# Eight experts' two-layer MLP on one core: float32 tokens loaded per expert beside the weights, and the last three experts regrouped by layer

## The chip, the core and the metric

The kernel runs on one core of a Trainium2 chip. The metric is the device time of one execution in microseconds (us); before the change the median of three runs is 189.09 us (189.03 to 189.41). The profile is one further execution, taken by the hardware profiler: its span, from the first to the last instruction, is 187.0 us. A core has TensorE (PE, matrix multiplication, with weight loads listed apart as PEld), VectorE (DVE), ScalarE (ACT), GpSimd (POOL) and SyncE (SP, which here only issues transfers). Data moves between the memory of the chip and the core's SBUF through 16 DMA engines, which the queues of all issuing engines share.

## The reference

```python
n_experts, capacity, hidden, expert_hidden = 8, 256, 512, 2048
def reference(x, w1, w2):          # all float32
    h = np.matmul(x, w1)           # [8,256,512] x [8,512,2048]
    h = np.maximum(h, 0)
    return np.matmul(h, w2).astype(np.float32)   # x [8,2048,512]
```

Each expert has 256 tokens of its own, a first weight matrix of 512 by 2048 and a second of 2048 by 512. In float32 each weight matrix is 4.19 MB, and the tokens of all experts together are another 4.19 MB. So seventeen portions of that size are read, and 4.19 MB are written.

## The kernel before

The work is cut into 128 rows (P). Everything is multiplied in bfloat16 and accumulated in float32 in PSUM.

*Loads.* Loads of x and of the weights are all issued by GpSimd, on one queue, and the transfer itself turns float32 into bfloat16. The order is x of all experts in one transfer (L47), and then for each expert its w1 (L52) and its w2 (L55). The last expert's w2 comes in four pieces (L58). The pool of weight tiles holds four w1 and four w2, so the load for expert e waits until the layer of expert e-4 that reads the same buffer is done.

*Transposes.* [...] All of x is transposed once, ahead of the first expert: 64 transposes of 128x128 (L72), gathered by eight into a PSUM tile, and eight copies to `xt_sb`, shared between VectorE (L82) and ScalarE (L80).

*First layer of expert e* (L91). There are eight groups of eight matmuls, each 128 columns of w1 against the 256 tokens. A group fills one of four PSUM tiles `pt_h`. The relu takes it to `ht_sb` in bfloat16, on ScalarE for even groups (L101) and on VectorE for odd ones (L99).

*Second layer of expert e* (L111). Two PSUM tiles `pt_o`, one for each half of the tokens, are accumulated over sixteen blocks of the inner dimension: 32 matmuls of 128x512. VectorE copies one half out (L119), ScalarE the other (L120). SyncE issues the store (L122). For the last expert each half has a store of its own (L124 on SyncE, L125 on ScalarE).

*Order.* Each engine carries out its own instructions in the order in which they stand in its program, and waits on semaphores. That order isn't simply the order of the source: [...] In the kernel before, the order that results on TensorE is the plain one, first layer and second layer of each expert in turn.

## Time and profile before

| | before |
|---|---|
| device time, median of 3 | 189.09 us |
| span of the profile | 187.0 us |
| TensorE matmuls busy | 133.5 us (71%) |
| VectorE busy, ScalarE busy | 32.6 us (17%), 29.1 us (16%) |
| read from memory, written | 71.30 MB, 4.19 MB |
| first layers: 512 matmuls, L91 | 60.6 us |
| second layers: 256 matmuls, L111 | 66.7 us |
| median from issue to landing, weight tile | 73.4 us |
| median from issue to landing, store of one expert | 15.1 us |

The table is read with one thing in mind: a busy share is an average over the whole span. The time from issue to landing includes the time that a transfer stands behind others in its queue; a weight tile's 73 us say that it is issued several tiles ahead, not that it takes that long to move. The profile's waits tell which engine stood still for what, and the chain of waits tells what the end of the run depended on.

### The profile page before, as it was taken

The page shows a single profiled execution, that of the slowest core. Times are in us where ns is not written, and L with a number is a line of the kernel's source. Part 1 is how long each engine was busy: PE and PEld are TensorE (multiplying, and loading weights), DVE is VectorE, ACT ScalarE, POOL GpSimd, SP SyncE. Part 2 cuts the span into 40 slices and gives each one's busy share as a digit, 9 for nine tenths or more (in the row PEclk, how much of TensorE's full clock was granted, in tenths as well). Part 3 has the DMA queues.
Part 4 walks back from the last instruction along what each step waited for, and adds up shares of the span by engine and source line. Part 5 has one row for each costly group of instructions (what it writes and reads, how often), then busy time and mean ns, then how long its engine had stood idle before and what let it go on. Part 6 is the DMA issues. An engine that isn't in the chain of part 4 may idle for free.

```text
span 187.0 us, 1874 instructions
## 1 busy us (share of the span) xinstructions
PE 133.5 (71%) x832; PEld 91.0 (49%) x832; DVE 32.6 (17%) x44; ACT 29.1 (16%) x45; POOL 11.4 (6%) x26
## 2 busy tenths in 40 slices
PE   0009399786949493899749992999659492979990
PEld 0009388335934293348713592348624491339740
DVE  0005404010410122002400141003300041012201
ACT  2004413011210131003200131003200230012201
POOL 7301000010010101001100200001000000000000
PEclk9999969996999999589966998599999999699999
DMA  4999999999999999999999999999999999999902
GB/s 70 214 221 224 224 217 214 203 210 235 215 273 214 207 241 223 240 224 217 214 245 221 224 244 231 239 200 207 258 245 225 213 234 226 224 207 233 236 18 112
DMA packets 4182, 39.95 MB, mean 214 GB/s; under 512 B 464, under 2 KB 464, under 8 KB 2128
## 3 DMA queue, kind: packets, MB, share of 16 engines
q0 software_dynamic: 2880, 35.65, 90.1%
q1 hardware_dynamic: 1152, 3.93, 5.6%
q10 hardware_dynamic: 144, 0.26, 0.4%
q8 instruction: 6, 0.10, 0.2%
HBM read 71.30 MB, written 4.19 MB: 404 GB/s over the span
## 4 chain that ended last, share of the span: by engine, by line
PE 60%; DMA 22%; another core or an unknown queue 14%; issue 1%; POOL 1%; ACT 0%; POOLq 0%
PE pt_o L111 32%; PE pt_h L91 28%; DMA w_sb<-in_w_dram 22%; POOL x_sb L47 0%; ACT out_sb L120 0%; POOL w_sb L52 0%; POOL identity masks.py:197 0%; POOL w_sb L55 0%; POOLq L140 0%
## 5 line engine op out<-in xcount | busy, mean ns | idle before, releaser
L111 PE MATMUL pt_o<-w_sb,ht_sb 128*128 128x512 bf16 x256 | 66.7, 426 | 22.3 <-DMA w_sb<-in_w_dram 22.3
L91 PE MATMUL pt_h<-xt_sb,w_sb 128*128 128x256 bf16 x512 | 60.6, 281 | 12.6 <-DMA w_sb<-in_w_dram 12.6
L91 PEld LDWEIGHTS <-w_sb 128*128 128x128 bf16 x512 | 57.4, 146 | 17.4 <-DMA w_sb<-in_w_dram 16.1
L111 PEld LDWEIGHTS <-ht_sb 128*128 128x128 bf16 x256 | 27.5, 107 | 59.6 <-issue 37.1
L99 DVE TENSOR_SCALAR ht_sb<-pt_h 128x512 bf16<-128x512 f32 x32 | 22.1, 692 | 52.4 <-PE pt_h L91 52.4
L101 ACT ACTIVATE ht_sb<-pt_h 128x512 bf16<-128x512 f32 x32 | 19.1, 597 | 46.6 <-PE pt_h L91 46.6
L119 DVE COPY out_sb<-pt_o 128x512 f32<-128x512 f32 x8 | 5.5, 692 | 81.6 <-PE pt_o L111 81.6
L120 ACT COPY out_sb<-pt_o 128x512 f32<-128x512 f32 x8 | 4.7, 588 | 91.0 <-PE pt_o L111 91.0
L72 PE MATMUL pt_tr<-identity,x_sb 128*128 128x128 bf16 x64 | 6.5, 296 | 14.0 <-DMA x_sb<-in_x_dram 14.0
L72 PEld LDWEIGHTS <-x_sb 128*128 128x128 bf16 x64 | 6.3, 141 | 14.0 <-DMA x_sb<-in_x_dram 14.0
L82 DVE COPY xt_sb<-pt_tr 128x1024 bf16<-128x1024 bf16 x4 | 4.9, 1225 | 16.4 <-PE pt_tr L72 16.4
L52 POOL DMA_DIRECT2D w_sb<-in_w_dram x8 | 4.4, 544 | 44.3 <-PE pt_h L91 44.3
L80 ACT COPY xt_sb<-pt_tr 128x1024 bf16<-128x1024 bf16 x4 | 4.0, 1012 | 15.5 <-PE pt_tr L72 15.5
L55 POOL DMA_DIRECT2D w_sb<-in_w_dram x7 | 3.8, 546 | 38.7 <-PE pt_o L111 30.5
L58 POOL DMA_DIRECT2D w_sb<-in_w_dram x4 | 2.1, 532 | 32.0 <-DMA w_sb<-in_w_dram 19.3
L80 ACT ACT_TABLE_LOAD x1 | 1.3, 1283 | 0.7 <-PEq L140 0.7
L47 POOL DMA_DIRECT2D x_sb<-in_x_dram x1 | 0.7, 664 | 0.8 <-POOLq L140 0.8
masks.py:199 POOL TENSOR_SCALAR_AFFINE_SELECT identity<-identity 128x128 bf16<-128x128 bf16 x1 | 0.3, 333 | 0.1
masks.py:197 POOL MEMSET identity<- 128x128 bf16 x1 | 0.2, 244 | 0.0
L140 POOL MEMSET const-float32-0.0<- 128x1 f32 x1 | 0.1, 99 | 0.2 <-issue 0.2
L140 POOL MEMSET const-bfloat16-1.0<- 128x1 bf16 x1 | 0.1, 102 | 0.0
L140 POOL MEMSET const-uint8-127<- 128x1 uint8 x1 | 0.1, 102 | 0.0
(1 smaller groups left out, 0.1 us busy)
## 6 DMA issues: line engine op xcount, KB each, us to landing
w_sb<-in_w_dram POOLq DMA_DIRECT2D x15, 2048.0 KB, 73.4
out_dram<-out_sb SPq DMA_DIRECT2D x7, 512.0 KB, 15.1
x_sb<-in_x_dram POOLq DMA_DIRECT2D x1, 2048.0 KB, 12.7
w_sb<-in_w_dram POOLq DMA_DIRECT2D x1, 768.0 KB, 66.0
w_sb<-in_w_dram POOLq DMA_DIRECT2D x1, 640.0 KB, 69.7
w_sb<-in_w_dram POOLq DMA_DIRECT2D x1, 384.0 KB, 61.4
w_sb<-in_w_dram POOLq DMA_DIRECT2D x1, 256.0 KB, 52.4
out_dram<-out_sb SPq DMA_DIRECT2D x1, 256.0 KB, 2.0
```

The costliest lines, as they stand in the source:

```text
L52: nc.gpsimd.dma_start(a[:], w1_r[e])
L55: nc.gpsimd.dma_start(b[:], w2_r[e])
L58: nc.gpsimd.dma_start(b[:, lo:hi, :], w2_r[e, :, lo:hi, :])
L72: nc.tensor.transpose(pt[:, j2, :], x_sb[:, j2 * MT + mt, kt::KT1], identity[:])
L80: nc.scalar.copy(dst, src)
L82: nc.vector.tensor_copy(dst, src)
L91: nc.tensor.matmul(pt[:, i, :], w1_sb[e][:, kt, 2 * g + i::KT2], xt_sb[:, kt, e, :], start=(kt == 0), stop=(kt == KT1 - 1),)
L99: nc.vector.tensor_relu(ht_sb[:, 2 * g:2 * g + 2, :], pt[:])
L101: nc.scalar.activation(ht_sb[:, 2 * g:2 * g + 2, :], pt[:], mybir.ActivationFunctionType.Relu,)
L111: nc.tensor.matmul(po[mt][:], ht_sb[:, kt, mt * P:(mt + 1) * P], w2_sb[e][:, kt, :], start=(kt == 0), stop=(kt == KT2 - 1),)
L119: nc.vector.tensor_copy(out_sb[:, 0, :], po[0][:])
L120: nc.scalar.copy(out_sb[:, 1, :], po[1][:])
```

## The change

The tokens are no longer loaded whole and cast by the transfer. Each expert's tokens come as a float32 tile on SyncE's queue (`load_x`), four experts ahead, beside the weights on GpSimd's queue. `first_layer` casts the tile to bfloat16 on ScalarE, transposes it (eight transposes) and copies the result out of PSUM on VectorE, ahead of the expert's first layer. This is meant to let the weights start at once, without 4.19 MB of x ahead of them, and to take the transposes out of the beginning.

The order of layers is written in a list. For experts 0 to 4 it is first layer, second layer, as before. For the last three it is the first layers of experts 5, 6 and 7 and then their second layers, and the loads follow the same list. It is meant to have only second layers left when the last weights arrive. The pool of hidden tiles grows from two to four buffers for this. Last, the final four matmuls of the last expert are reordered so that the first half of its tokens is finished two matmuls earlier.

The core of the diff:

```diff
-    x_sb = const.tile([P, J, H], bf, name="x_sb")
-    nc.gpsimd.dma_start(x_sb[:], x_r)
...
-    hpool = ctx.enter_context(tc.tile_pool(name="hidden", bufs=2))
+    xpool = ctx.enter_context(tc.tile_pool(name="xs", bufs=AHEAD))
+    tpool = ctx.enter_context(tc.tile_pool(name="xts", bufs=2))
+    hpool = ctx.enter_context(tc.tile_pool(name="hidden", bufs=4))
...
+    def load_x(e):
+        x_sb[e] = xpool.tile([P, MT, H], f32, tag="x", name="x_sb")
+        nc.sync.dma_start(x_sb[e][:], x_r[e])
...
+    def first_layer(e):
+        x_bf = tpool.tile([P, MT, H], bf, tag="xb", name="x_bf")
+        nc.scalar.copy(x_bf[:], x_sb[e][:])
+        pt = ps_o.tile([P, KT1, MT, P], bf, tag="ps_o", name="pt_tr")
         for kt in range(KT1):
+            for mt in range(MT):
                 nc.tensor.transpose(
+                    pt[:, kt, mt, :], x_bf[:, mt, kt::KT1], identity[:]
                 )
+        xt = tpool.tile([P, KT1, C], bf, tag="xt", name="xt_sb")
+        nc.vector.tensor_copy(xt[:], pt[:].rearrange("p k m q -> p k (m q)"))
...
+        if last:
+            order = order[:-4] + [(kt, mt) for mt in range(MT) for kt in (KT2 - 2, KT2 - 1)]
...
+    order = []
+    for e in range(E - 3):
+        order += [(1, e), (2, e)]
+    order += [(1, e) for e in range(E - 3, E)] + [(2, e) for e in range(E - 3, E)]
+
+    for e in range(AHEAD):
+        load_x(e)
+    for layer, e in order:
+        (load_w1 if layer == 1 else load_w2)(e)
...
+    for layer, e in order:
+        if layer == 1:
+            first_layer(e)
+        else:
+            second_layer(e)
+            if e + AHEAD < E:
+                load_x(e + AHEAD)
```

## The prediction

> **What bounds the kernel now.** I read the page's slices first, then the chain of waits, then TensorE's timeline, and last the stretches between landings. The slices, 4.675 us each:

> ```profile
> PE   0009399786949493899749992999659492979990
> DMA  4999999999999999999999999999999999999902
> GB/s 70 214 221 224 224 217 214 203 210 235 215 273 214 207 241 223 240 224 217 214 245 221 224 244 231 239 200 207 258 245 225 213 234 226 224 207 233 236 18 112
> ```

> The DMA row is full from the second slice to the 38th; TensorE's row has holes everywhere. The transfers set the pace until about 178 us, and what comes after is a tail. The chain of waits shows the tail:

> ```profile
> 158.50 8.75 PE pt_o L111 x32
> 167.26 0.99 another core or an unknown queue
> 168.25 0.04 issue
> 168.29 7.21 PE pt_h L91 x64
> 175.50 6.92 PE pt_o L111 x32
> 182.42 0.02 issue
> 182.44 0.59 ACT out_sb L120
> ```

> At 168.25 the last w1 lands. From there TensorE works without a stop: 7.21 + 6.92 us. The last weights land near 178 us while it is still busy, so the end hangs on the landing before last, plus two layers. From the last matmul (182.42) to the end of the span (187.0) are 4.58 us of eviction, store and closing.

> TensorE's timeline shows how a layer's length depends on the idle time ahead of it (in brackets):

> ```profile
> 55.17 7.07 PE L111 MATMUL pt_o<-w_sb,ht_sb 128*128 128x512 bf16 x32 [2.61 <-DMA w_sb<-in_w_dram]
> 75.49 9.87 PE L111 MATMUL pt_o<-w_sb,ht_sb 128*128 128x512 bf16 x32 [3.66 <-DMA w_sb<-in_w_dram]
> 95.84 9.93 PE L111 MATMUL pt_o<-w_sb,ht_sb 128*128 128x512 bf16 x32 [3.32 <-DMA w_sb<-in_w_dram]
> 147.60 7.20 PE L91 MATMUL pt_h<-xt_sb,w_sb 128*128 128x256 bf16 x64 [2.75 <-DMA w_sb<-in_w_dram]
> 158.50 8.75 PE L111 MATMUL pt_o<-w_sb,ht_sb 128*128 128x512 bf16 x32 [3.69 <-DMA w_sb<-in_w_dram]
> ```

> The same 32 matmuls take 7.07 us after 2.6 us of idling and up to 9.93 us after more than 3.3: the clock had been halved. The stretches between landings (length, busy times by engine, clock, DMA share, GB/s written) give the price of a weight tile:

> ```profile
> 147.56:158.46 10.90, 7.20 (x64) 7.04 (x65) 2.77 (x4) 2.39 (x4) 0.00 (x0) 1.00 1.02 240
> 158.46:168.25 9.79, 8.75 (x32) 3.46 (x31) 0.69 (x1) 0.59 (x1) 0.00 (x0) 0.83 0.97 206
> ```

> A tile takes 9.8 us; the stretch that also carries a store takes 10.9, so a store of 0.52 MB costs 1.1.

> [...]

> **The change part by part.**

> *Bytes.* Nothing is saved: x is read as 4.19 MB of float32 either way. In before x is one portion on the queue of the weights, about 9.8 us. As plain float32 it moves like the stores do. By stretches that is 8 x 1.1 = 8.8 us; by the page's queue table the 3.93 MB of q1 took 5.6% of 187 us, so 4.19 MB take 11.2. I take 10.0, that is +0.2, and keep -1.0 and +1.4.

> *Start.* SyncE is released at about 0.7 us, GpSimd issued x at 1.23. I take -0.5 us (bounds 0 and -1.2, as the first GB/s show in before only after 2.5 us).

> *Casts, transposes, copies.* Eight casts on ScalarE: nearest row L80, 128x1024 at 1.01 us, so 8.1 us instead of the 4.0 of its transposing copies. VectorE: eight copies at L82's 1.23 us, 9.8 instead of 4.9. TensorE keeps its 64 transposes. Both engines are busy under a fifth of the span, so this hides beside the weights. One wait is awkward: in the built order of ScalarE the cast of expert 2 stands ahead of the first relu of expert 0. Its x lands late: an engine has 8 packets of a weight tile (128 rows over 16 engines), 9.8/8 = 1.2 us each, and with one packet of x between them an x tile lands every 11 us or so; if the first is in by 4 us, the third is in by 26. TensorE fills its four PSUM tiles and then waits, and finishes expert 0's first layer near 32 us, where before it finished at 32.3 (29.81 + 2.46). It catches up by over 2 us on every tile (7.1 to 7.2 against 9.8). Loads of weights don't starve: they are issued four experts ahead. Cost nothing, hidden behind transfers.

> *Order of layers, as written.* It buys little. After the landing before last (now w2 of expert 6) two layers remain, as before: 7.07 + 6.92 against 7.21 + 6.92. The gain would be that this landing has one store fewer ahead of it (-1.1).

> *Order of layers, as built.* Here is the bulk. The built program's order on TensorE near the end isn't that of the list:

> ```
> first layer 5, first layer 6 (waits for its w1)
> 8 transposes of expert 7
> second layer 5: 5 matmuls, the first waits for w2 of expert 5
> first layer 7: 64 matmuls (waits for its w1)
> second layer 5: the other 27 matmuls
> second layer 6, second layer 7
> ```

> The scheduler put five matmuls of second layer 5 ahead of first layer 7. But w2 of expert 5 is queued behind w1 of expert 7, so it lands about 9.8 us later. Matmuls being in program order, first layer 7 stands with its weights landed behind a wait for the next tile. After first layer 6 TensorE idles for 2 x 9.8 - 7.2 = 12.4 us, and then owes four layers while only two tiles are still under way.

> *The sum.* Landing of w2 of expert 5: before, 168.25 is the landing of the 16th portion, with six stores ahead. Now w2 of expert 5 is the 15th (x and 14 tiles), with five stores: 168.25 - 9.8 - 1.1 - 0.5 (start) + 0.2 (x) = 157.05. Then, at full clock, 5 x 0.216 = 1.1, first layer 7.2, 27 x 0.216 = 5.8, and 6.92 twice: 27.95 us. The clock is halved at the beginning, after 12 us of idling. Rows of before lose 1.5 (8.75 against 7.21, first layer at 43.81) to 2.9 us (9.93 - 7.07). [...] I take 2.5. The last tiles land at 157.05 + 9.8 = 166.9 and about 178, while second layer 6 can begin only at 157.05 + 2.5 + 14.1 = 173.6 and second layer 7 at 180.6: no more waits. Last matmul 187.5. The tail of 4.58 stays, as ScalarE's half still ends last; the reordered four matmuls only free SyncE's store 0.43 us earlier. I take 4.55. Span 192.05; the measured time lies 2.09 above the span (189.09 - 187.0): 194.1.

> **The rivals.**
> 1. *TensorE isn't held.* If first layer 7 runs at the landing of its w1, only the start, x and one store count: the landing before last at 168.25 - 1.1 - 0.5 + 0.2 = 166.85, then the same tail, -1.4 in all: 187.7 us, faster. For it: the source says so. Against: the built order, and matmuls in program order.
> 2. *The hold is there, and x is dear.* Small float32 packets between the weights slow the whole stream: x at its upper bound, no gain at the start: +1.7, so 195.8. For it: q1's 11.2 us. Against: the stores' 1.1 us.
> 3. *The hold is there, and cheap.* Short warm-up (1.7) and x at 8.8: -2.0, so 192.1. For it: the slow row that lost only 1.5.
> 4. *No change*, 189: the hold is paid back by a much better start. The transfers are full from the second slice on, so there is nothing of 5 us to be had.

> **How the numbers follow.** The forecast, 194.1, has 0.62; dear x 0.15; the cheap hold 0.15; TensorE not held 0.06; no change 0.02. The 80% range spans the held cases: low 191.7 and high 196.3. Slower 0.92, same 0.02, faster 0.06.

> **What would show it.** In the profile after: an idle TensorE of some 12 us before the second layer's first matmuls near 157 us, put down to a weight transfer, and then one busy stretch of about 30 us to the end; a low clock at its beginning; the DMA row full until about 178 and then empty for some 9 us; w2 of expert 7 landed long before it is read. x tiles landing some 11 us apart would confirm the alternation. It is wrong if the first layer of expert 7 runs near 148 us, or if the DMA row has gaps earlier.

## The result, and the profile after

The changed kernel takes 193.56 us (median of four runs, 193.39 to 193.78) against 189.13 us for the kernel before beside it: a ratio of 1.0233, 95% interval 1.0215 to 1.025. It is slower by 4.4 us. The span of the profile is 191.8 us.

The slices of the page, now 4.8 us each:

```profile
PE   0204969489591978669492956998395029999990
PEclk9999999969999699969999997899879856999997
DMA  7999999999999999999999899999999999998113
GB/s 253 220 220 259 220 259 222 256 218 260 214 264 214 263 212 263 215 256 221 253 220 262 206 262 222 219 198 256 224 220 215 219 219 219 204 209 212 45 66 111
```

The transfers are as full as before, up to about 177 us. After them TensorE is busy for two slices, about 10 us, with no load under way. Well ahead of that TensorE is hardly busy (5, 0 and 2 tenths in the slices from 143.8 to 158.2 us), and the clock is low in the slices from 153.4 to 163.0 us (5 and 6). The chain of waits puts times on them (start, length, what):

```profile
146.70 9.99 another core or an unknown queue
156.69 0.04 issue
156.73 0.59 PE pt_o L103
157.31 0.22 issue
157.53 1.49 PE pt_o L103 x3
159.02 8.41 PE pt_h L79 x64
167.43 0.05 issue
167.49 10.74 PE pt_o L103 x49
178.23 0.05 issue
178.28 8.81 PE pt_o L103 x40
187.09 0.03 ACTq L112
```

TensorE stands still for 10 us, runs the first matmuls of second layer 5 (L103), then all of first layer 7 (L79), then the rest. From 156.69 to the end it never waits for a transfer again. TensorE's timeline names the releaser of the idle time:

```profile
137.38 8.88 PE L79 MATMUL pt_h<-xt_sb,w_sb 128*128 128x256 bf16 x64 [3.67 <-DMA w_sb<-in_w_dram]
146.09 0.61 PE L68 MATMUL pt_tr<-identity,x_bf 128*128 128x128 bf16 x8
156.73 0.59 PE L103 MATMUL pt_o<-w_sb,ht_sb 128*128 128x512 bf16 x1 [10.03 <-DMA w_sb<-in_w_dram]
```

The 10.03 us are a wait of the second layer (L103) for its weights. The landings in the trace show w1 of expert 7 complete at 147.0 us: first layer 7 had its weights for those 10 us and stood behind a matmul that didn't. The granted clock of the stretches from there (the last three columns are clock, DMA share, GB/s):

```profile
147.30:156.69 9.39, 0.00 (x0) 0.00 (x0) 0.27 (x1) 0.00 (x0) 0.00 (x0) 0.73 1.05 223
156.69:161.00 4.31, 4.05 (x15) 2.45 (x16) 0.00 (x0) 0.19 (x1) 0.00 (x0) 0.50 0.94 201
161.00:167.40 6.40, 6.40 (x55) 6.17 (x55) 2.07 (x3) 2.20 (x4) 0.00 (x0) 0.94 0.99 208
```

The four owed layers begin at half clock (0.50). The last weights land at 176.23 us, 3.2 us earlier than in the kernel before (179.39), and yet the kernel ends later: with the hold, the last landing isn't what the end hangs on.

### The profile page after: what moved, and what is told of

It reads as the page before. It is cut to its first block, busy times and chain, and to the rows that moved or that the text cites. A ratio compares the mean times of both kernels' runs of the same rounds, so it can differ in the third digit from the quotient of the medians.

```text
span 191.8 us, 1891 instructions
## 1 busy us (share of the span) xinstructions
PE 130.0 (68%) x824; PEld 91.5 (48%) x832; DVE 32.7 (17%) x48; ACT 33.0 (17%) x49; POOL 10.8 (6%) x25
## 3 DMA queue, kind: packets, MB, share of 16 engines
q1 hardware_dynamic: 2304, 8.13, 11.2%
HBM read 71.30 MB, written 4.19 MB: 394 GB/s over the span
## 4 chain that ended last, share of the span: by engine, by line
PE 54%; DMA 24%; another core or an unknown queue 17%; POOL 1%; issue 1%; DVE 0%; ACT 0%; POOLq 0%; ACTq 0%
PE pt_o L103 27%; PE pt_h L79 26%; DMA w_sb<-in_w_dram 24%; PE pt_tr L68 1%; POOL w_sb L54 0%; DVE xt_sb L72 0%; ACT out_sb L112 0%; POOL w_sb L60 0%; POOL identity masks.py:199 0%; POOL identity masks.py:197 0%; POOLq masks.py:199 0%; ACTq L112 0%; POOLq L153 0%
## 5 line engine op out<-in xcount | busy, mean ns | idle before, releaser
L79 PE MATMUL pt_h<-xt_sb,w_sb 128*128 128x256 bf16 x512 | 67.7, 301 | 29.7 <-DMA w_sb<-in_w_dram 29.4
L79 PEld LDWEIGHTS <-w_sb 128*128 128x128 bf16 x512 | 61.7, 149 | 35.9 <-DMA w_sb<-in_w_dram 30.8
L103 PE MATMUL pt_o<-w_sb,ht_sb 128*128 128x512 bf16 x248 | 58.4, 391 | 22.2 <-DMA w_sb<-in_w_dram 21.6
L103 PEld LDWEIGHTS <-ht_sb 128*128 128x128 bf16 x256 | 25.6, 100 | 52.9 <-issue 25.6
L111 DVE COPY out_sb<-pt_o 128x512 f32<-128x512 f32 x8 | 5.5, 692 | 61.3 <-PE pt_o L103 61.3
L64 ACT CAST x_bf<-x_sb 128x1024 bf16<-128x1024 f32 x8 | 8.4, 1045 | 13.3 <-DMA x_sb<-in_x_dram 13.3
L68 PE MATMUL pt_tr<-identity,x_bf 128*128 128x128 bf16 x64 | 5.1, 231 | 5.1 <-ACT x_bf L64 5.1
L68 PEld LDWEIGHTS <-x_bf 128*128 128x128 bf16 x64 | 4.6, 117 | 6.2 <-ACT x_bf L64 5.1
L72 DVE COPY xt_sb<-pt_tr 128x1024 bf16<-128x1024 bf16 x8 | 5.4, 688 | 6.2 <-PE pt_tr L68 6.2
```

What stands on the lines that cost most here:

```text
L64: nc.scalar.copy(x_bf[:], x_sb[e][:])
L68: nc.tensor.transpose(pt[:, kt, mt, :], x_bf[:, mt, kt::KT1], identity[:])
L72: nc.vector.tensor_copy(xt[:], pt[:].rearrange("p k m q -> p k (m q)"))
L79: nc.tensor.matmul(ph[:, i, :], w1_sb[e][:, kt, 2 * g + i::KT2], xt[:, kt, :], start=(kt == 0), stop=(kt == KT1 - 1),)
L103: nc.tensor.matmul(po[mt][:], ht[e][:, kt, mt * P:(mt + 1) * P], w2_sb[e][:, kt, :], start=(kt == 0), stop=(kt == KT2 - 1),)
L111: nc.vector.tensor_copy(o[:, 0, :], po[0][:])
```

## The experiments

Each runs beside the kernel before on the same chip (189.12 to 189.15 us). Edits are shown against the changed kernel, in experiment 3 against the kernel before; `...` marks lines left out. Times of landing are the DMA completions in the traces.

**1. The list's order kept on TensorE.** The first two matmuls of each second layer are tied behind everything that the source has ahead of them on TensorE. In the timeline below the waits are for data alone (1.03, 1.64 and 2.65 us).

```diff
-        for kt, mt in order:
-            nc.tensor.matmul(
+        for i, (kt, mt) in enumerate(order):
+            mm = nc.tensor.matmul(
...
+            if i < MT:
+                tc.keep_in_program_order(mm)
```

> The changed kernel with one difference: on TensorE the second layer of expert 5 is kept behind the first layer of expert 7, as the list of layers has it. Theory (the hold costs the time): first layer 7 runs when its w1 lands near 147 us, no idle stretch of 10 us, the landing of w2 of expert 6 near 166.5 us is followed by two layers (14 us) and the tail of 4.6: span about 185.2, time about 187.2 us. Rival (float32 x, or the regrouping as such, costs the time): it stays at 193 to 194 us.

Measured: 186.73 us, ratio 0.9896 (0.9851 to 0.9941); three runs lie at 186.6 to 186.9, one at 188.5. Its timeline of TensorE:

```profile
147.81 7.19 PE L79 MATMUL pt_h<-xt_sb,w_sb 128*128 128x256 bf16 x64 [1.03 <-DVE xt_sb L72]
156.64 7.07 PE L103 MATMUL pt_o<-w_sb,ht_sb 128*128 128x512 bf16 x32 [1.64 <-DMA w_sb<-in_w_dram]
166.36 13.97 PE L103 MATMUL pt_o<-w_sb,ht_sb 128*128 128x512 bf16 x64 [2.65 <-DMA w_sb<-in_w_dram]
```

First layer 7 now fills the hole, and w2 of expert 5 lands where it did in the changed kernel (156.59 against 156.69). Only the order on TensorE differs, and 6.8 us are gone. The place of the five matmuls is the cause of the loss, and without it the change is faster than the kernel before.

**2. The x part alone.** The list is first layer, second layer for all experts. The four hidden buffers and the reordered last four matmuls stay.

```diff
-    for e in range(E - 3):
+    for e in range(E):
         order += [(1, e), (2, e)]
-    order += [(1, e) for e in range(E - 3, E)] + [(2, e) for e in range(E - 3, E)]
```

> The x part of the change alone: x per expert in float32, but first and second layer of each expert in turn to the end, so no hold in TensorE's order. Theory (x costs about what it did, and the start gains half a microsecond): w1 of expert 7 lands within 1 us of the 168.25 of the kernel before, time 188.0 to 189.1 us. Rival (small float32 packets make x dear): 190 to 191 us.

Measured: 190.23 us, ratio 1.0056 (1.0039 to 1.0072). The time is the rival's, but not by the rival's mechanism: the landing agreed with the theory (w1 of expert 7 at 168.09, against 168.25 before), and TensorE's last layer ended at 182.25, against 182.40 before. The microsecond was lost behind it: from there to the end of the span took 6.2 us instead of 4.6. The timeline of its end:

```profile
181.91 0.69 DVE L111 COPY out_sb<-pt_o 128x512 f32<-128x512 f32 x1 [5.84 <-PE pt_o L103]
182.63 0.33 SPq L114 DMA_DIRECT2D out_dram<-out_sb  x1
182.64 0.59 ACT L112 COPY out_sb<-pt_o 128x512 f32<-128x512 f32 x1 [7.54 <-DVE out_sb L111]
183.26 1.86 ACTq L115 DMA_DIRECT2D out_dram<-out_sb  x1
```

ScalarE's issue of the last store took 1.86 us, where before and in the changed kernel it took 0.37. Experiment 6 follows this up.

**3. The regrouping alone.** The kernel before, with the list of layers for loads and layers and four hidden tiles; x comes in one transfer as before.

```diff
-    hpool = ctx.enter_context(tc.tile_pool(name="hidden", bufs=2))
+    hpool = ctx.enter_context(tc.tile_pool(name="hidden", bufs=4))
...
+    order += [(1, e) for e in range(E - 3, E)] + [(2, e) for e in range(E - 3, E)]
...
+    for layer, e in order:
+        (first_layer if layer == 1 else second_layer)(e)
```

> The regrouping alone: the kernel before with its x in one transfer, and the first layers of experts 5 to 7 ahead of their second layers, in loads and layers. Its built order on TensorE is that of the list, without the five matmuls ahead of first layer 7. Theory (the regrouping itself only moves one store behind the landing before last): about 1 us faster than before, 188.0 us. Rival (the regrouping itself costs): 192 us or more.

Measured: 187.73 us, ratio 0.9942 (0.9924 to 0.996); four of the twenty runs lie at 189.2 to 189.7, and the profile is of one of these. In it w2 of expert 6 lands at 166.98, where before the landing before last came at 168.25. The regrouping gains 1.4 us, about what the displaced store costs. The five matmuls aren't ahead of first layer 7 in this build, nor in the x part's, where that first layer is nowhere near them: the hold appears only where both parts stand together. Why the built order has them there was not looked into.

**4. The hold left, the clock kept up.** Forty matmuls without use between the transposes of expert 7 and the held ones; everything else stands in TensorE's order as in the changed kernel, for which second layer 5 is split into its first five matmuls and the rest and tied in that order. What the forty compute isn't read.

```diff
+        if e == E - 1:
+            fill = ps_o.tile([P, H], f32, tag="ps_o", name="pt_fill")
+            for i in range(FILL):
+                tc.keep_in_program_order(nc.tensor.matmul(
+                    fill[:], identity[:], w1_sb[e - 1][:, 0, :H], start=True, stop=True
+                ))
+            second_layer(E - 3, 0, 5)
...
+    FILL = 40
```

> The changed kernel with its hold left in place, instruction for instruction, and 40 matmuls of 128x512 without use added on TensorE in the 10 us before w2 of expert 5 lands, so that its clock isn't halved when the four owed layers begin. They compute nothing that is kept. Theory (2.4 us of the tail is half-rate clock, the rest is the hold): 2.4 us under the changed kernel, about 191.2 us. Rival (the clock costs nothing, all of it is the hold): 193.6 us.

Measured: 190.93 us, ratio 1.0113 (1.008 to 1.0146). The chain of waits of this kernel:

```profile
146.39 8.63 PE pt_fill L78 x40
155.02 1.62 another core or an unknown queue
156.64 0.04 issue
156.69 1.24 PE pt_o L117 x5
157.92 6.99 PE pt_h L86 x64
164.91 19.66 PE pt_o L117 x91
184.56 0.03 ACTq L130
```

The stretch after the landing, at a clock of 1.00 where the changed kernel had 0.50:

```profile
156.69:161.00 4.31, 4.31 (x35) 3.76 (x35) 0.69 (x1) 1.02 (x2) 0.00 (x0) 1.00 0.98 209
```

The same work after the same landing takes 27.9 us instead of 30.4. So of the 6.8 us that the hold costs, 2.6 are half-rate clock (193.56 - 190.93), and 4.2 are the first layer moved behind the landing (190.93 - 186.73). The profiles agree on the second: 6.99 us of matmuls, less the idle 2.65 us that experiment 1 still had between two second layers, are 4.3.

**5. The last four matmuls in plain order.**

```diff
-        if last:
-            order = order[:-4] + [(kt, mt) for mt in range(MT) for kt in (KT2 - 2, KT2 - 1)]
```

> The changed kernel with the last expert's final four matmuls in plain order. Theory (the end hangs on ScalarE's half, which ends with the last matmul either way): within 0.2 us of the changed kernel, 193.4 to 193.8 us. Rival (the earlier first half saves its 0.43 us): 194.0 us.

Measured: 193.55 us (193.06 to 194.66), against 193.56. The runs spread too far to tell 0.4 us apart, but the traces do: from the last matmul to the end of the span both kernels take 4.7 us. In the plain order SyncE issues its half of the store 0.6 us after the last matmul, in the other 0.4 us after it; ScalarE's half is issued 0.7 us after it in both, and lands last (190.46 after 189.85 in the changed kernel). So the reordering saves nothing.

**6. The x part alone, with six short instructions more on ScalarE.** The list is as in experiment 2; shown is what is added to that.

```diff
+        if e == 0:
+            pad = const.tile([P, 1], f32, name="pad")
+            for i in range(6):
+                nc.scalar.copy(pad[:], x_sb[0][:, 0, i:i + 1])
```

> The x part alone, with six copies of 128x1 added on ScalarE ahead of its first relu; they compute nothing that is kept. In the run without them the issue of ScalarE's last store took 1.86 us instead of 0.37, with an 8 KB transfer of instructions starting just then (183.3 us), and the eviction ahead of it began 0.3 us late. Theory (ScalarE fetched instructions just at its last store; six instructions more move that to an earlier place): the issue takes 0.37 us again, 188.7 to 189.1 us. Rival (float32 x itself makes the end longer): 190.2 us as before.

Measured: 188.65 us, ratio 0.9967 (0.9955 to 0.9979). More instructions, and 1.6 us less. The timeline of its end, ScalarE alone:

```profile
182.27 0.58 ACT L116 COPY out_sb<-pt_o 128x512 f32<-128x512 f32 x1 [7.23 <-PE pt_o L107]
182.88 0.37 ACTq L119 DMA_DIRECT2D out_dram<-out_sb  x1
```

That the six instructions remove the long issue is shown (0.37 us instead of 1.86); that ScalarE waited for the transfer of instructions is the author's theory, and wasn't shown. Such a transfer alone isn't enough: in the changed kernel one of 8 KB started at 187.86 us, within ScalarE's issue of the last store (187.77), and the issue took its 0.37 us. The trace doesn't tell whose instructions were moved. So float32 x isn't dear, and experiment 2's extra microsecond was none of x.

**7. w2 of expert 6 in pieces.** The list's order kept as in experiment 1, and expert 6's w2 loaded in the four pieces of expert 7's.

```diff
-        cuts = (0, KT2) if e < E - 1 else (0, 6, 11, 14, 16)
+        cuts = (0, KT2) if e < E - 2 else (0, 6, 11, 14, 16)
```

> The kernel with the layers kept in the order of the list, and w2 of expert 6 loaded in the same four pieces as w2 of expert 7, so that its second layer runs while it arrives. Theory (TensorE still works 14 us after the landing before last, and the weights end near 177 us): the second layer of expert 6 ends about 1 us after its last piece, the last matmul follows the last piece of expert 7 near 178 us by 1 to 2 us; 185.5 to 186.3 us, up to 1 us under the 186.73 of the kernel in list order. Rival (extra pieces slow the transfers, or the clock halves in the gaps between pieces and takes it back): 186.7 us or more.

Measured: 186.24 us, ratio 0.9848 (0.9834 to 0.9863), half a microsecond under experiment 1.

```profile
157.19 22.57 PE L103 MATMUL pt_o<-w_sb,ht_sb 128*128 128x512 bf16 x96 [2.79 <-DMA w_sb<-in_w_dram]
```

The theory's time, but not by its reasons: TensorE ran its 96 last matmuls without a stop from 157.19, at a clock of 0.61 in the first 4 us, and ended at 179.77, 1.8 us after the last piece. The bound had moved to the landing of w2 of expert 5.

**8. Two stores behind the weights.** As 7, with the stores of experts 5 and 6 on GpSimd's queue.

```diff
-            nc.sync.dma_start(out_r[e], o[:])
+            (nc.gpsimd if e >= E - 3 else nc.sync).dma_start(out_r[e], o[:])
```

> As the kernel with w2 of expert 6 in pieces, and in addition the stores of experts 5 and 6 issued on GpSimd's queue, behind the last weights instead of between them. Theory (the end hangs on the last landing of weights, which these two stores push out by about 1 us each): the last weights land near 176 us, 184 to 185 us. Rival (the two stores, now last, collide with the last expert's store): no faster than with the stores between the weights.

Measured: 184.55 us, ratio 0.9758 (0.9717 to 0.9799). The runs fell into two groups, 183.8 and 185.3 us, so the median lies in the expected range and no run does. The last weights landed at 176.31, in experiment 7 at 178.01. The chain of waits of the profiled run, which was of the first group:

```profile
156.96 0.04 issue
157.00 20.89 PE pt_o L103 x96
177.89 0.03 ACTq L114
```

So here too TensorE ran from the landing of w2 of expert 5 without a stop, and the last landing, on which the theory had the end hang, isn't on the chain. What the two stores are worth is therefore not separated. The 96 matmuls took 20.9 us at full clock against 22.6 in experiment 7, and from the last matmul to the end of the span it was 4.1 us against 4.6. The earlier landing was needed all the same: the first group's last matmul, at 177.88, came before experiment 7's last weights.

**9. The same again, on another chip.**

> The kernel with the stores of experts 5 and 6 behind the weights, once more beside the one above and on its chip. Theory: two groups near 183.8 and 185.3 us. Rival (the groups were an accident of one chip): one group.

Measured: runs at 183.6 and 183.9, at 185.3 and 185.5, and two at 187.1; ratio 0.9761 (0.9727 to 0.9795) without the last two. These are three groups, one more than expected. The profile is of a run at 187.1. Its clock from 157 us on, and below it that of experiment 8:

```profile
157.00:161.00 4.00, 3.44 (x8) 1.28 (x9) 0.00 (x0) 0.00 (x0) 0.53 (x1) 0.50 1.04 213
157.00:161.00 4.00, 4.00 (x19) 1.84 (x19) 0.00 (x0) 0.00 (x0) 0.53 (x1) 1.00 1.04 214
```

The clock of the slow run is 0.92 from 154 to 157 us, 0.50 to 161 and 0.71 to 165. If it was at half without a break, that is from about 156.5 to 163.3 us, of which TensorE works through 6.0 us, from 157.34 on: by this estimate a loss of 3.0 us. Its 96 matmuls took 23.8 us against 20.9. The shortest stretch of half clock in the traces of the kernel before and of the changed one is 3.41 us; TensorE at work all through one more of these would lose half of it, 1.7 us. This estimate fits the steps between the groups, 1.6 and 1.7 us; the middle group wasn't profiled.

**10. w2 of experts 5 to 7 in pieces.** As 8, and expert 5's w2 in the same pieces.

```diff
-        cuts = (0, KT2) if e < E - 1 else (0, 6, 11, 14, 16)
+        cuts = (0, KT2) if e < E - 3 else (0, 6, 11, 14, 16)
```

> As the kernel with the stores of experts 5 and 6 behind the weights, with w2 of expert 5 in the same four pieces too, so that TensorE has about 8 us of slack in its last 28 us of work. The runs of the kernel without this fell into two groups, 183.8 and 185.3 us. Theory (TensorE's 96 last matmuls were its bound, 20.9 us from the landing of w2 of expert 5, and one more stretch of halved clock in them made the second group): last matmul about 1 us after the last piece near 176.3 us, 183.0 to 183.9 us, and a slow stretch of clock is mostly absorbed, so one group. Rival (the last stores or the transfers made the groups): the same two groups, 184.5 us median.

Measured: 184.13 us (184.10, 184.11, 184.14, 184.71), ratio 0.9744 (0.9731 to 0.9756). The time lies 0.2 above the range: the last piece landed at 176.56 instead of 176.3, and the last matmul came 1.4 us after it, not 1.

```profile
154.98 13.98 PE L103 MATMUL pt_o<-w_sb,ht_sb 128*128 128x512 bf16 x62
```

The groups are gone, as far as four runs can tell. The theory put this to TensorE's slack, but the profile offers a second reason: second layer 5 now follows first layer 7 without the idle stretch of some 3 us that stood there in experiments 8 and 9, and the clock is 1.00 in every stretch looked at from 150 to 178 us. The run doesn't separate the two. By its median this is the fastest kernel of the study, 9.4 us under the changed one; the first groups of experiments 8 and 9 are 0.2 to 0.5 us faster still.

## Why the prediction was right

*Landing of w2 of expert 5.* Predicted 157.05, measured 156.69. The difference by portions and stores held within 0.4 us, although the first data of x moved at 1.8 us and those of the weights only at 4.6. The first two x tiles used that gap. The x part's own balance is 0.3 us by the reckoning. In experiment 6 w1 of expert 7 lands at 168.02 instead of 168.25, 0.2 us earlier, and the span is no shorter (186.9 in the profiled run, 187.0 before). The 0.5 us by which that kernel's time lies under the kernel before are outside the span, which the prediction didn't reckon with: the measured time lies 1.8 us above the span with x on SyncE's queue, and 2.3 us above it in the kernel before.

*The hold.* Predicted from the built order and from the author's assumption that matmuls stay in program order; the timeline shows it (first layer 7, its w1 landed at 147.0 us, runs at 159.02, behind matmuls that waited for the landing at 156.69), and experiment 1 takes it away. The idle stretch is 10.0 us, not 12.4: first layer 6 itself ran slow, 8.88 us after an idle 3.67, and the transposes took another 0.45. These 2.4 us lie ahead of the landing, so the miss didn't move the end.

*Work after the landing.* Predicted 27.95 us at full clock and 2.5 for the warm-up, 30.45 in all. Measured: 30.40 (187.09 - 156.69). Experiment 4 separates the terms: 27.9 and 2.5. That the warm-up came out at 2.5 is in part luck. The clock is 0.50 until 161.8 us, 5.1 us after the work began, which loses 2.5; in experiment 5, with the same hold, the same work took 29.9 us, a loss of 2.0. Where the half clock would end was not foreseen; the 2.5 was the author's estimate, between the 1.5 and the 2.9 us that rows of the kernel before lose.

*Tail.* 4.55 predicted, 4.7 measured; span 192.05 against 191.8. The measured time lies 1.8 us above the span, 2.09 were used. (Those 2.09 set the median of other runs against the span of the profiled one, which itself took 189.31 us.) All terms but the tail err to the same side, and together make the 0.5 us of 194.1 against 193.56.

*The clock.* The prediction reads its lines as a clock that is halved by an idle stretch of over 3.3 us. Its own profile has a line that goes against this, the first below, and the changed kernel has two with the same idle stretch and different lengths:

```profile
137.79 7.07 PE L111 MATMUL pt_o<-w_sb,ht_sb 128*128 128x512 bf16 x32 [3.87 <-DMA w_sb<-in_w_dram]
83.38 8.79 PE L79 MATMUL pt_h<-xt_sb,w_sb 128*128 128x256 bf16 x64 [3.51 <-DMA w_sb<-in_w_dram]
105.54 7.21 PE L79 MATMUL pt_h<-xt_sb,w_sb 128*128 128x256 bf16 x64 [3.51 <-DMA w_sb<-in_w_dram]
```

The clock was 1.00 through the first and the third; in the second it was 0.50 from 83.31 to 86.72 us. In the line of 9.87 us that the prediction shows, it was 0.50 from 75.49 to 81.19. So half clock goes with the long lines, but the idle time just ahead of a layer doesn't tell its length. After the hold's 10 us TensorE was slow in both traces that have it: the clock of the changed kernel was 0.50, and in experiment 5 the five matmuls ahead of first layer 7 took 2.29 us, where at a clock of 1.00 they took 1.24 (experiment 4). So the forecast didn't hang on this.

*The rivals.* The kernel not held was put at 187.7 and measures 186.73; the sign was right, and its landing before last came at 166.31 instead of 166.85. Dear x falls with experiment 6. The cheap hold, 192.1, needed a warm-up of 1.7 us and x at 8.8; the warm-up was 2.5 us, and 2.0 in experiment 5.

*What hid.* Two side estimates were too pessimistic, without consequence. ScalarE's cast of expert 2 was to wait until 26 us; ScalarE's timeline has it at 17.46:

```profile
4.04 1.04 ACT L64 CAST x_bf<-x_sb 128x1024 bf16<-128x1024 f32 x1 [2.02 <-DMA x_sb<-in_x_dram]
5.26 1.05 ACT L64 CAST x_bf<-x_sb 128x1024 bf16<-128x1024 f32 x1 [0.18 <-DMA x_sb<-in_x_dram]
17.46 1.05 ACT L64 CAST x_bf<-x_sb 128x1024 bf16<-128x1024 f32 x1 [11.15 <-DMA x_sb<-in_x_dram]
```

Two x tiles, not one, came in ahead of the weights. From then on the alternation was as the author had estimated: from 6.0 to 17.5 us 154 packets of the weights' queue and 150 of x's moved, and the next tiles landed at 17.4, 28.4, 39.4 and 50.4 us, each 0.2 to 0.3 us after a weight tile. The first layer of expert 0 ended at 26.6 instead of 32. And VectorE's copies of the transposed x took 688 ns each, not the 1225 of the row that they were priced by. That row writes its tile in a strided order; whether this makes the difference wasn't tested.

## What to carry to other kernels

Read the order that was built, not only the order that was written: one matmul whose input lands later, placed ahead of one whose input is there, held TensorE for 10.0 us here, and it doesn't show in the source. In a kernel that waits for its transfers, the end hangs on the last landing that has more work behind it than the rest of the transfers takes (in the changed kernel the one at 156.69 us, with 30.4 us of work behind it and 19.5 of transfers). Loads in pieces shorten that work (experiment 7, 186.24 us against 186.73), and stores put behind the last loads bring the last landing forward (experiment 8, from 178.01 to 176.31 us), which helps only where the end hangs on it. An idle stretch on TensorE can be paid twice, once as idle time and once as slow clock after it, and the second part remains when the first is hidden: with the idle 10 us filled by work without use, experiment 4 was 2.6 us faster.
